# The GLU of branch A as a branch of the tail, and another order of the tail's branches

## The chip, the cores and the metric

The kernel runs on one core of one Trainium2 chip. The metric is device microseconds of one execution of the whole program. Three executions of the kernel before took 1948.1, 1957.22 and 1959.81 us (median 1957.22); a fourth was recorded by the hardware profiler and took 1951.2 us.

## The reference, cut to what matters

One layer of an encoder with four token mixers. `x` has 1024 prompt rows and 128 sample rows (T = 1152 together), 1024 columns, float32.

```python
h = split_cols(x @ p['w_in'])
ya, s5_re, s5_im = s5_branch(h['a_u'], p, st)         # A: state space, GELU, then the GLU below
yb, ... = dsa_branch(h, rel_bias, st)                 # B: sparse attention
yc, ... = gdn_branch(h, p, st)                        # C: gated DeltaNet
yd, ... = gla_branch(h, p, st)                        # D: GLA
branches = stack([ya * silu(a_gate), yb * silu(b_gate), yc * silu(c_gate), yd * silu(d_gate)])
proj  = einsum('ntbw,bwd->ntbd', branches, p['w_branch'])
gates = sigmoid(h['merge'])                           # (n, t, 4, 1024)
mixed = sum_b(gates * proj) @ p['w_out']
x = layer_norm(alpha * x + mixed)

# the end of s5_branch
y = gelu(y)                                           # (n, t, 512)
g = y @ p['s5_w_glu']                                 # (n, t, 1024)
ya = g[..., :512] * sigmoid(g[..., 512:])
```

## The kernel before, in words

Every product of two float32 matrices is made of three matmuls in a rounded format: `split` writes a rounded high part of a tile (ACT, L111 with a scale, L108 without) and the rest as a low part (DVE, L112 and L109), and `mm3` multiplies high by high (L188), high by low (L189) and low by high (L190). A product of a 128-column weight block with 384 tokens and 512 inner elements is thus 4 x 3 = 12 matmuls into one PSUM tile; the texts call it a **group**.

The tail starts when the projections are done. For each branch, `mix_branch` loads the branch's gated output `y_b` ... `y_a` from DRAM in three chunks of 384 tokens (tile `yl`, 768 KB each, two buffers), splits each into `YH` and `YL`, and then goes through eight blocks of 128 output columns: load and split a block of `w_branch` (`wst`, `whi`, `wlo`), three groups (`mix`, one for each chunk), and for each group a load of the merge gate (`mth`, three buffers), one DVE multiplication (L1769, or L1767 straight into the sum in the first branch) and one DVE addition into the sum `ACC` (L1770). Groups of one branch take their PSUM tiles in turn from two pools of two (`pg` and `pn`), so a group can start only when the one four before it was multiplied by DVE. One branch is 24 groups. The order of the branches is b, c, d, a; `finish` then multiplies the sum by `w_out` (`fin`) and normalises.

`YH` and `YL` have four places for chunks: one in the pool `y0`, opened early, three in `yb`. A branch's second and third chunk are split only when the branch before has used up a place, near its end.

`s5_glu` makes `y_a`. It reads the GELU output (`s5_y`, 512 x 1152) in four loads of 128 rows (`gy`), splits each with the tokens put in order on the way (`GH`, `GL`), and runs 24 groups (`glu`), two at a time (value and gate); ACT takes tanh of the gate (L1684), DVE combines twice (L1685, L1686), the second time with the branch's own gate (`glgt`), and the result is stored to `y_a`. Its tiles lie in pools on the right side of SBUF, where GLA (branch D) has its own until it ends.

The instructions are put in order by a scheduler that goes by priority: program order, with a class above it (`urgent`: loads and splits) and one below (`filler`). It decides while the program is built, so on the chip each engine and each DMA queue works its list strictly in order. GLA is still running through the first two branches of the tail: its last chunk of tokens goes through seven levels (`gla_levels`: DVE makes `X` and `glZ`, ACT an exponential, PE `lv` at L1208, DVE puts the result into `glAT` at L1211, after a first L1182), between `rms_gate` (L1062, PE `py` at L1065, DVE `oyt` at L1067) of the chunk before and its own.

Almost all DMAs are issued by one engine's queue, SP, each in its place of the list: one that waits holds up all behind it.

Of the kernel before, what the change touches and what calls it, by code (L numbers as in the profile page):

```python
# [95 lines left out]
def pmt(K, name="pm"):  # L96
    return K.pm.tile([128, 512], F32, tag="pm", name=name)
# [6 lines left out]
def split(K, hi, lo, src, scale=None, eng=None):  # L104

    nc = K.nc
    if scale is None:
        nc.scalar.copy(hi, src)  # L108
        (eng or nc.vector).tensor_tensor(lo, src, hi.bitcast(F32), op=OP.subtract)  # L109
    else:  # L110
        nc.scalar.activation(hi, src, AF.Copy, scale=scale)  # L111
        nc.vector.scalar_tensor_tensor(lo, src, scale, hi.bitcast(F32), op0=OP.mult, op1=OP.subtract)  # L112
# [1541 lines left out]
                nc.sync.dma_start(dst, t[:n, d * 64:d * 64 + 64])  # L1654


def s5_glu(K):

    nc, tc, I = K.nc, K.tc, K.I
    with tc.tile_pool(name="glu1", bufs=1, side="right") as p1, tc.tile_pool(name="glu", bufs=2, side="right") as p, \  # L1660
            tc.tile_pool(name="wglu", bufs=2, side="right") as wg:
        GH = p1.tile([128, 4, T], F32R, name="GH")
        GL = p1.tile([128, 4, T], F32R, name="GL")
        for j in range(4):
            y = p.tile([128, 8, 144], F32, name="gy", bufs=3)
            nc.sync.dma_start(y.rearrange("p s k -> p (s k)"), K.YA[j * 128:j * 128 + 128])
            o = lambda x: x[:, j].rearrange("p (k s) -> p s k", s=8)
            split(K, o(GH), o(GL), y, scale=0.5)
        for j in range(4):
            wv = load_w(K, [(j * 128, 128, 0), (512 + j * 128, 128, 128)], 256, kt=4, src=I["s5_w_glu"], pool=wg, stage=wg)  # L1670
            hi, lo = wv
            for t0 in range(0, T, 384):
                s = slice(t0, t0 + 384)
                pp = []
                for a in range(2):
                    ps = pmt(K, "glu")
                    ca = slice(a * 128, a * 128 + 128)
                    for k in range(4):
                        mm3(nc, ps[:, :384], hi[:, k, ca], lo[:, k, ca], GH[:, k, s], GL[:, k, s], k == 0, k == 3)
                    pp.append(ps)  # L1680
                th = p.tile([128, 384], F32, name="glth")
                gt = p.tile([128, 384], F32, name="glgt")
                nc.sync.dma_start(gt, K.GD["a"][j * 128:j * 128 + 128, s])
                nc.scalar.activation(th, pp[1][:, :384], AF.Tanh, scale=0.5)  # L1684
                nc.vector.scalar_tensor_tensor(th, th, 1.0, pp[0][:, :384], op0=OP.add, op1=OP.mult)  # L1685
                nc.vector.scalar_tensor_tensor(th, th, 0.5, gt, op0=OP.mult, op1=OP.mult)  # L1686
                nc.sync.dma_start(K.YD["a"][j * 128:j * 128 + 128, s], th)


def s5(K):  # L1690
    nc, tc = K.nc, K.tc
    with tc.tile_pool(name="sp", bufs=1) as K.sp:
# [25 lines left out]
    gemm_t(K, w, K.XH, K.XL, evac)  # L1718


def mix_branch(K, n, br, yp, p):

    nc, I = K.nc, K.I
    YH, YL, W = [], [], []

    def load_y(c):
        pool = K.y0 if (3 * n + c) % 4 == 0 else yp
        YH.append(pool.tile([128, 4, 384], F32R, tag="YH", name="YH"))
        YL.append(pool.tile([128, 4, 384], F32R, tag="YL", name="YL"))
        src = K.YD[br].rearrange("(k p) t -> p k t", p=128)[:, :, c * 384:c * 384 + 384]  # L1730
        if n == 0 and c == 0:
            for k in (slice(0, 2), slice(2, 4)):
                y = K.ws.tile([128, 1024], F32, tag="wst", name="yl")[:, 0:768].rearrange("p (k t) -> p k t", k=2)
                nc.sync.dma_start(y, src[:, k])
                split(K, YH[c][:, k], YL[c][:, k], y, scale=0.5)
            return
        y = p.tile([128, 4, 384], F32, tag="yl", name="yl")
        d = nc.sync.dma_start(y, src)
        if n == 0:
            K.ydma = d  # L1740
        split(K, YH[c], YL[c], y, scale=0.5)

    def load(dt):
        W.append(load_w(K, [(dt * 128, 128, 0)], 128, kt=4, src=I["w_branch"][BR[br]]))
    with urgent(K):
        for c in range(3):
            load_y(c)
            if c < 2:
                load(c)
    c = 0  # L1750
    for dt in range(8):
        if n == 3:
            w_out_part(K, dt, p)
        if dt > 1:
            load(dt)
        hi, lo = W[dt]
        for t in range(3):
            s = slice(t * 384, t * 384 + 384)
            ps = (K.pg.tile([128, 512], F32, tag="pg", name="mix") if c % 2 else pnt(K, "mix"))[:, :384]
            c += 1  # L1760
            for k in range(4):
                mm3(nc, ps, hi[:, k], lo[:, k], YH[t][:, k], YL[t][:, k], k == 0, k == 3)
            th = p.tile([128, 384], F32, tag="mth", name="mth", bufs=3)
            nc.sync.dma_start(th, K.MD[br][dt][:, s])
            a = K.ACC[:, dt, s].bitcast(F32)
            if n == 0:
                nc.vector.scalar_tensor_tensor(a, th, 1.0, ps, op0=OP.add, op1=OP.mult)  # L1767
            else:
                nc.vector.scalar_tensor_tensor(th, th, 1.0, ps, op0=OP.add, op1=OP.mult)  # L1769
                nc.vector.tensor_tensor(a, a, th, op=OP.add)  # L1770


def tail(K):
    tc = K.tc
    with tc.tile_pool(name="mx", bufs=2) as p, tc.tile_pool(name="ap", bufs=1) as ap, \
            tc.tile_pool(name="yb", bufs=3) as yp:
        K.ACC = ap.tile([128, 8, T], F32R, name="ACC")
        s5_glu(K)
        K.wo = K.ctx.enter_context(tc.tile_pool(name="wo", bufs=1, side="right"))
        mix_branch(K, 0, "b", yp, p)  # L1780
        mix_branch(K, 1, "c", yp, p)
        mix_branch(K, 2, "d", yp, p)
        mix_branch(K, 3, "a", yp, p)
        finish(K, yp, p)


# [157 lines left out]
def build(ctx, tc, I, O, stages, dev=None):  # L1944
    K = Env()
    K.nc, K.tc, K.ctx, K.I, K.O = tc.nc, tc, ctx, I, O
    setup(K)
    K.GD = {b: K.dram.tile([512, T], F32, name=f"gate_{b}") for b in "abcd"}
    K.YD = {b: K.dram.tile([512, T], F32, name=f"y_{b}") for b in "abcd"}
    K.MD = {b: [K.dram.tile([128, T], F32, name=f"merge_{b}{j}") for j in range(8)] for b in "abcd"}  # L1950
    K.QD = K.dram.tile([768, T], F32, name="q_d")
    K.VD = K.dram.tile([T, 512], F32, name="gla_v")
    K.UD = K.dram.tile([512, T], F32, name="s5_u")
    K.YA = K.dram.tile([512, T], F32, name="s5_y")
    K.DQK = [K.dram.tile([128, T], F32, name=f"dqk{a}") for a in range(4)]
    K.CQ = [K.dram.tile([512, T], F32, name=f"cq{a}") for a in range(3)]
    K.gp = ctx.enter_context(tc.tile_pool(name="gp", bufs=2))
    K.ws = ctx.enter_context(tc.tile_pool(name="ws", bufs=2))
    K.wp = ctx.enter_context(tc.tile_pool(name="wp", bufs=2))
    with tc.tile_pool(name="xp", bufs=1) as K.xp, ExitStack() as wn, ExitStack() as nat:  # L1960
        K.wn = wn.enter_context(tc.tile_pool(name="wn", bufs=1, side="right"))
        K.wnp = nat.enter_context(tc.tile_pool(name="wnat", bufs=1, side="right"))
        load_x(K)
        with tc.tile_pool(name="cvc", bufs=1) as K.cvc:
            gdn_prepare(K)
            K.glmask = gla_masks(K)
            with tc.tile_pool(name="bp", bufs=1) as K.bp:
                with ExitStack() as cv:
                    natural_cols(K)
                    nat.close()  # L1970
                    project_q(K)

                    def between():
                        project_rest(K, "end" in stages)
                        wn.close()
                        K.cvp = cv.enter_context(tc.tile_pool(name="cvp", bufs=2, side="right"))
                        project(K, "end" in stages)
                    dsa(K, between)
            if "c" in stages:
                gdn(K)  # L1980
            gdn_conv_state(K)
            if "a" in stages:
                s5(K)
            if "end" in stages:
                K.y0 = ctx.enter_context(tc.tile_pool(name="y0", bufs=1, side="right"))
            if "d" in stages:
                gla(K)
    if "end" in stages:
        tail(K)
    elif "a" in stages:  # L1990
        s5_glu(K)
    if dev:
        dev(K)

# [16 lines left out]
```

## Time and profile before

| | us |
|---|---|
| profiled execution | 1951.2 |
| its span in the trace | 1949.4 |
| median of 3 other executions | 1957.22 |
| PE busy (matmuls) | 1826.5 (94%) |
| DVE busy | 1450.9 (74%) |
| ACT busy | 681.0 (35%) |
| `mix` matmuls | 1512.1 to 1841.3 |
| `glu` matmuls | 1688.1 to 1746.3 |
| `fin` matmuls | from 1841.3 |

Times inside the execution are microseconds from the start of the span. A window row gives, for a stretch, the busy time of each engine with the number of its instructions, then the clock granted to the matmul engine as a share of full speed (1.00 is 2.4 GHz, 0.50 is 1.2 GHz), the busy share of the 16 DMA engines and their GB/s. A busy matmul engine at half clock is still busy, so the number of matmuls in a window tells what was done. A timeline row gives start, duration, engine, line, operation, written tile <- read tiles; in brackets the idle time before it and what ended it.

### The profile page before, as it was taken

The numbers are of one execution on the slowest core, as the hardware profiler recorded it, in microseconds if no ns is written. First come the engines' busy times: TensorE is split into PE (matmuls) and PEld (weight loads), VectorE is DVE, ScalarE is ACT, GpSimd is POOL, SyncE is SP. The second block draws the span as 40 slices with busy tenths as digits, with TensorE's granted clock in tenths as the row PEclk, the third lists the DMA queues.
The fourth block names the chain that finished last, engine by engine and source line by source line (L and its number), as shares of the span: only waits on it lengthen the run. The fifth ranks groups of instructions, "written<-read, shape, count | busy, mean of one in ns | idle before, by whom it ended". The sixth has DMA issues, their size and how long they took to land.

```text
span 1949.4 us, 31176 instructions
## 1 busy us (share of the span) xinstructions
PE 1826.5 (94%) x10962; PEld 1711.5 (88%) x10962; DVE 1450.9 (74%) x3915; ACT 681.0 (35%) x1538; POOL 265.7 (14%) x297
## 2 busy tenths in 40 slices
PE   7999999999999999988889898888898999899997
PEld 7989999989888999888888787778888899899986
DVE  7289999944999995489740669977657889747676
ACT  4251111133666655264212333223532322412210
POOL 1110111210212110101111112212212000000000
PEclk9999999999999999999998999999999999899999
DMA  6322323223222222386334554444353544656522
GB/s 191 96 68 70 88 85 97 91 90 86 82 82 67 73 59 79 81 269 192 102 94 139 152 149 126 143 125 132 123 134 104 179 130 146 192 169 192 159 87 87
DMA packets 333386, 234.53 MB, mean 120 GB/s; under 512 B 70475, under 2 KB 315003, under 8 KB 333230
## 3 DMA queue, kind: packets, MB, share of 16 engines
q1 hardware_dynamic: 325358, 220.87, 38.6%
q10 hardware_dynamic: 7488, 10.62, 1.5%
q8 instruction: 87, 1.43, 0.3%
q0 software_dynamic: 384, 1.05, 0.2%
q14 instruction: 69, 0.57, 0.1%
HBM read 156.12 MB, written 76.35 MB: 119 GB/s over the span
## 4 chain that ended last, share of the span: by engine, by line
PE 34%; DVE 16%; DMA 5%; issue 4%; ACT 3%; POOL 1%; SPq 1%; DVEq 0%; POOLq 0%; ACTq 0%
PE pg L190 3%; PE pg L188 3%; PE pg L189 3%; PE mix L189 2%; PE mix L188 2%; PE mix L190 2%; PE fin L190 2%; PE fin L188 2%; PE fin L189 2%; PE lv L1208 1%; PE glu L189 1%; PE glu L190 1%; PE glu L188 1%; DMA P<-rows_d 1%; DVE glAT L1211 1%
## 5 line engine op out<-in xcount | busy, mean ns | idle before, releaser
L190 PE MATMUL pg<-XH,wlo 128*128 128x384 f32 x1648 | 566.6, 344 | 0.0
L188 PE MATMUL pg<-XH,whi 128*128 128x384 f32 x1648 | 564.6, 343 | 1.9 <-DVE gth L237 1.9
L189 PE MATMUL pg<-XL,whi 128*128 128x384 f32 x1648 | 565.8, 343 | 0.0
L188 PEld LDWEIGHTS pg<-XH,whi 128*128 128x128 f32 x1648 | 314.3, 191 | 5.8 <-DVE gth L237 2.4
L190 PEld LDWEIGHTS pg<-XH,wlo 128*128 128x128 f32 x1648 | 314.2, 191 | 3.9 <-issue 1.8
L189 PEld LDWEIGHTS pg<-XL,whi 128*128 128x128 f32 x1648 | 313.9, 190 | 4.0 <-issue 2.0
L108 ACT CAST whi<-wst 128x1024 fp32r<-128x1024 f32 (+2 forms) x121 | 109.2, 906 | 243.9 <-PE pg L189 122.5
L109 POOL TENSOR_TENSOR wlo<-wst,whi 128x1024 fp32r<-128x1024 f32 x44 | 109.3, 2485 | 371.2 <-ACT whi L108 345.0
L109 DVE TENSOR_TENSOR wlo<-wst,whi 128x512 fp32r<-128x512 f32 (+2 forms) x77 | 74.7, 974 | 83.6 <-ACT whi L108 82.1
L189 PE MATMUL mix<-YL,whi 128*128 128x384 f32 x384 | 130.6, 341 | 1.5 <-DVE YL L112 1.4
L188 PE MATMUL mix<-YH,whi 128*128 128x384 f32 x384 | 130.7, 341 | 0.8 <-ACT YH L111 0.6
L190 PE MATMUL mix<-YH,wlo 128*128 128x384 f32 x384 | 131.2, 342 | 0.0
L1716 ACT ACTIVATE mth<-pg 128x384 f32<-128x384 f32 x96 | 46.9, 488 | 151.7 <-PE pg L190 88.0
L391 DVE TENSOR_SCALAR_CACHE_REDUCE tkj<-mk,tk_c 128x384 bf16<-128x384 f32 (+6 forms) x112 | 90.9, 875 | 0.6
L391 DVE TENSOR_SCALAR_CACHE_REDUCE tkj<-tkh,tk_c 128x384 bf16<-128x384 bf16 (+6 forms) x112 | 90.9, 876 | 0.5
L189 PEld LDWEIGHTS mix<-YL,whi 128*128 128x128 f32 x384 | 72.4, 189 | 2.2 <-DVE YL L112 2.1
L188 PEld LDWEIGHTS mix<-YH,whi 128*128 128x128 f32 x384 | 72.3, 188 | 1.7 <-ACT YH L111 0.9
L714 DVE SCALAR_TENSOR_TENSOR cy<-rb,cw,cy 128x384 f32<-128x384 f32 (+1 forms) x108 | 70.8, 656 | 3.0 <-ACT cy L712 2.5
L190 PEld LDWEIGHTS mix<-YH,wlo 128*128 128x128 f32 x384 | 72.5, 189 | 0.2
L534 ACT ACTIVATE pr<-pr,sm 128x256 f32<-128x256 f32 (+7 forms) x72 | 53.6, 745 | 16.9 <-DVE sm L533 16.5
L501 POOL TENSOR_TENSOR mb<-BT,mk 128x512 f32<-128x512 f32 (+1 forms) x32 | 42.0, 1313 | 107.8 <-DVE mx L528 102.5
L190 PE MATMUL fin<-WOH,YL 128*128 128x512 f32 x144 | 56.0, 389 | 0.0
(632 smaller groups left out, 3786.2 us busy)
## 6 DMA issues: line engine op xcount, KB each, us to landing
wst<-in_w_in SPq DMA_DIRECT2D x80, 512.0 KB
wst<-in_w_branch SPq DMA_DIRECT2D x32, 256.0 KB
gk<-cq SPq DMA_DIRECT2D x27, 256.0 KB
merge_b<-mth SPq DMA_DIRECT2D x24, 192.0 KB
cq<-cy SPq DMA_DIRECT2D x24, 192.0 KB
merge_c<-mth SPq DMA_DIRECT2D x24, 192.0 KB
kq<-cq SPq DMA_DIRECT2D x18, 256.0 KB
merge_d<-mth SPq DMA_DIRECT2D x24, 192.0 KB
```

The source lines that it names most:

```text
L108: nc.scalar.copy(hi, src)
L109: (eng or nc.vector).tensor_tensor(lo, src, hi.bitcast(F32), op=OP.subtract)
L188: nc.tensor.matmul(ps, lh, rh, start=start, stop=False)
L189: nc.tensor.matmul(ps, lh, rl, start=False, stop=False)
L190: return nc.tensor.matmul(ps, ll, rh, start=False, stop=stop)
L391: nc.vector.tensor_scalar(junk[a % 2][:, :ns[a]], up[a] if bit > 15 else sc[a], cand[:, a:a + 1].bitcast(F32), None, op0=OP.is_ge, op1=OP.add,
L501: bias = nc.gpsimd.tensor_tensor(mbv, bt[:, 2 * jj:2 * jj + 2, ::-1][:, :, 256 - band:], mk[:, None, off:n].to_broadcast([128, 2, band]), ...
L534: nc.scalar.activation(p[:, r, 0:n], p[:, r, 0:n], AF.Exp, bias=sm[:, 2 + r:3 + r], scale=1.0, accum_out=sm[:, r:r + 1])
L714: nc.vector.scalar_tensor_tensor(yc, rb[:, i:i + c], K.cw[:, i * 12 + a:i * 12 + a + 1], yc, op0=OP.mult, op1=OP.add)
L1208: nc.tensor.matmul(ps[:, o:o + 128], x[:, j, z * 128:z * 128 + 128], Z[:, j, :, z * 64:z * 64 + 64], start=True, stop=True)
L1211: nc.vector.copy_predicated(right(AT[:, 0:m].rearrange("p i h t -> p (i h) t")), right(masks[l][:, None, :]).to_broadcast([128, 4 * m, 64 ...
L1716: nc.scalar.activation(th[:, :n], ps, AF.Tanh, scale=0.5)
```

## The change

The GLU is written as one more branch: it uses the four `YH`/`YL` places, the `yl`, `mth` and `gth` buffers, the weight buffers and the two PSUM pools that the branches use. The GELU output stays in its stored order of tokens within a chunk (t mod 8 outer, t div 8 inner), so a chunk is loaded by four DMAs of 128 rows x 8 pieces x 48 elements (192 bytes a piece) and split without reordering; the order is put right in the last DVE operation. Gate and value groups alternate by block: three gate groups, tanh of each kept, then three value groups. The order of the branches becomes b, c, GLU, a, d, and `w_out` is loaded during d.

```diff
-def s5_glu(K):
...
+def load_y(K, n, c, yp):
+    pool = K.y0 if (3 * n + c) % 4 == 0 else yp
+    return [pool.tile([128, 4, 384], F32R, tag=t, name=t) for t in ("YH", "YL")]
+
+def filler_psum(K, c, name):
+    return (K.pg.tile([128, 512], F32, tag="pg", name=name) if c % 2 else pnt(K, name))[:, :384]
+
+def s5_glu(K, n, yp, p):
+    nc, I = K.nc, K.I
+    Y, W = [], []
+    def load(x):
+        W.append(load_w(K, [((1 - x % 2) * 512 + x // 2 * 128, 128, 0)], 128, kt=4, src=I["s5_w_glu"]))
+    with urgent(K):
+        for c in range(3):
+            Y.append(load_y(K, n, c, yp))
+            y = p.tile([128, 4, 384], F32, tag="yl", name="gy")
+            for k in range(4):
+                nc.sync.dma_start(y[:, k].rearrange("p (s t) -> p s t", s=8),
+                                  K.YA[k * 128:k * 128 + 128].rearrange("p (s t) -> p s t", s=8)[:, :, c * 48:c * 48 + 48])
+            split(K, Y[c][0], Y[c][1], y, scale=0.5)
+            if c < 2:
+                load(c)
+    c = 0
+    th = [None] * 3
+    for x in range(8):
+        j = x // 2
+        if x > 1:
+            load(x)
+        hi, lo = W[x]
+        for t in range(3):
+            s = slice(t * 384, t * 384 + 384)
+            ps = filler_psum(K, c, "glu")
+            c += 1
+            for k in range(4):
+                mm3(nc, ps, hi[:, k], lo[:, k], Y[t][0][:, k], Y[t][1][:, k], k == 0, k == 3)
+            if x % 2 == 0:
+                th[t] = p.tile([128, 384], F32, tag="mth", name="glth", bufs=3)
+                nc.scalar.activation(th[t], ps, AF.Tanh, scale=0.5)
+                continue
+            gt = K.gp.tile([128, 384], F32, tag="gth", name="glgt")
+            nc.sync.dma_start(gt, K.GD["a"][j * 128:j * 128 + 128, s])
+            nc.vector.scalar_tensor_tensor(th[t], th[t], 1.0, ps, op0=OP.add, op1=OP.mult)
+            g = gt.rearrange("p (t s) -> p t s", s=8)
+            nc.vector.scalar_tensor_tensor(g, th[t].rearrange("p (s t) -> p t s", s=8), 0.5, g, op0=OP.mult, op1=OP.mult)
+            nc.sync.dma_start(K.YD["a"][j * 128:j * 128 + 128, s], gt)
...
-        s5_glu(K)
         K.wo = K.ctx.enter_context(tc.tile_pool(name="wo", bufs=1, side="right"))
         mix_branch(K, 0, "b", yp, p)
         mix_branch(K, 1, "c", yp, p)
-        mix_branch(K, 2, "d", yp, p)
+        s5_glu(K, 2, yp, p)
         mix_branch(K, 3, "a", yp, p)
+        mix_branch(K, 4, "d", yp, p, last=True)
         finish(K, yp, p)
```

The order that the scheduler makes of it differs from b's end to the end of a. DVE at the start of branch c, before (`mth` and `mix` tiles of one group share a number's neighbourhood: 17763 is c's first group, 17780 its second; `YL_18208` is the split of d's first chunk):

```order
L1769 SCALAR_TENSOR_TENSOR mth_17776<-mth_17776,mix_17763 128x384
...
L1769 SCALAR_TENSOR_TENSOR mth_17793<-mth_17793,mix_17780 128x384
...
L112 SCALAR_TENSOR_TENSOR YL_18208<-yl_18209,YH_18207 128x1536
...
L1067 SCALAR_TENSOR_TENSOR oyt_16555<-py_16550,dnorm_15544,dgt_16504 128x512
...
L1182 TENSOR_TENSOR glAT_16566<-ident_70,diag_16569 128x1024
```

The same place now (17297 is c's first group, 17314 its second; `YL_17742` is the split of the GLU's first chunk):

```order
L1784 SCALAR_TENSOR_TENSOR mth_17310<-mth_17310,mix_17297 128x384
...
L1067 SCALAR_TENSOR_TENSOR oyt_16555<-py_16550,dnorm_15544,dgt_16504 128x512
...
L112 SCALAR_TENSOR_TENSOR YL_17742<-gy_17743,YH_17741 128x1536
...
L1182 TENSOR_TENSOR glAT_16566<-ident_70,diag_16569 128x1024
...
L1211 COPY_PREDICATED glAT_16566<-lm3_400,lv_16621 128x64x8
...
L1784 SCALAR_TENSOR_TENSOR mth_17327<-mth_17327,mix_17314 128x384
L1211 COPY_PREDICATED glAT_16566<-lm4_411,lv_16634 128x32x16
```

The multiplication of c's second group, which stood before GLA's `oyt` and L1182, now stands behind four of its levels.

SP at the end of the GLU, now (`glgt_18171`, `18189`, `18207` are the last three results, one for each chunk; `yl_18214`, `18226`, `18238` are the chunks of `y_a` for branch a):

```order
L1737 DMA y_a_91<-glgt_18171 128x384
L1779 DMA mth_18255<-merge_a0_95 128x384
L1737 DMA y_a_91<-glgt_18189 128x384
L1755 DMA yl_18214<-y_a_91 128x4x384
L1755 DMA yl_18226<-y_a_91 128x4x384
L181 DMA wst_18403<-in_w_branch 128x4x128
L1733 DMA glgt_18207<-gate_a_87 128x384
L1779 DMA mth_18272<-merge_a0_95 128x384
L1737 DMA y_a_91<-glgt_18207 128x384
L1779 DMA mth_18289<-merge_a0_95 128x384
L1755 DMA yl_18238<-y_a_91 128x4x384
```

Before, the same stores and loads stood beside branch d's remaining seven blocks; now branch a's loads follow the last store, and no group of another branch stands between them on PE.

PE at the end of the GLU, now (18194 is its last group; 18242, 18259 and 18276 are branch a's first block with its three chunks, 18293 the second block with the first chunk):

```order
L190 MATMUL glu_18194<-YH_17771,wlo_18153 128x384
L188 MATMUL mix_18242<-YH_18212,whi_18218 128x384
...
L188 MATMUL mix_18259<-YH_18224,whi_18218 128x384
L188 MATMUL mix_18293<-YH_18212,whi_18230 128x384
L189 MATMUL mix_18259<-YL_18225,whi_18218 128x384
...
L188 MATMUL mix_18276<-YH_18236,whi_18218 128x384
```

Before, 21 groups of branch d stood between the last `glu` matmul and the first of branch a.

## Rows read from the trace of the kernel before

**Rows 1.** The page, busy time of each engine over the span.
```profile
PE 1826.5 (94%) x10962; PEld 1711.5 (88%) x10962; DVE 1450.9 (74%) x3915; ACT 681.0 (35%) x1538; POOL 265.7 (14%) x297
```

**Rows 2.** Windows of the tail: PE, PEld, DVE, ACT, POOL, clock, DMA, GB/s.
```profile
1614.00:1648.00 34.00, 33.47 (x213) 31.99 (x212) 32.82 (x75) 7.26 (x12) 0.00 (x0) 1.00 0.49 147
...
1750.00:1787.00 37.00, 37.00 (x212) 37.00 (x211) 23.70 (x45) 3.96 (x7) 0.00 (x0) 1.00 0.58 188
```

**Rows 3.** Windows around the first matmuls of the GLU, same columns.
```profile
1683.00:1689.00 6.00, 3.02 (x12) 2.04 (x11) 3.32 (x3) 4.70 (x5) 0.00 (x0) 0.81 0.93 305
1689.00:1694.00 5.00, 5.00 (x19) 5.00 (x18) 4.27 (x3) 2.18 (x1) 0.00 (x0) 0.55 0.64 217
1694.00:1697.00 3.00, 2.37 (x14) 2.05 (x12) 0.69 (x1) 2.86 (x3) 0.00 (x0) 1.00 0.30 110
1697.00:1700.00 3.00, 1.43 (x7) 1.12 (x7) 2.90 (x2) 2.28 (x2) 0.00 (x0) 1.00 0.85 262
1700.00:1704.00 4.00, 4.00 (x16) 4.00 (x16) 3.29 (x4) 0.00 (x0) 0.00 (x0) 0.57 0.30 104
```

**Rows 4.** Waits of PE from 1500 on: total us, times, longest.
```profile
PE glu L188 <- ACT GH L111: 1.8, 2, 1.1
PE glu L189 <- DVE GL L112: 1.4, 1, 1.4
```

**Rows 5.** Timeline of SP: issues at three places of the tail.
```profile
1611.12 0.37 SPq L1738 DMA_DIRECT2D yl<-y_d  x1
...
1680.62 0.51 SPq L1666 DMA_DIRECT2D gy<-s_y  x1
...
1740.02 0.32 SPq L1687 DMA_DIRECT2D y_a<-glth  x1
...
1741.89 0.37 SPq L1738 DMA_DIRECT2D yl<-y_a  x1
...
1744.18 0.32 SPq L1687 DMA_DIRECT2D y_a<-glth  x1
```

**Rows 6.** Timeline of DVE through GLA's last chunk at the start of branch c.
```profile
1614.35 0.54 DVE L1769 SCALAR_TENSOR_TENSOR mth<-mth,mix 128x384 f32<-128x384 f32 x1
...
1616.30 0.55 DVE L1769 SCALAR_TENSOR_TENSOR mth<-mth,mix 128x384 f32<-128x384 f32 x1
...
1617.22 1.76 DVE L112 SCALAR_TENSOR_TENSOR YL<-yl,YH 128x1536 fp32r<-128x1536 f32 x1 [0.30 <-ACT YH L111]
...
1623.20 0.75 DVE L1067 SCALAR_TENSOR_TENSOR oyt<-py,dnorm,dgt 128x512 f32<-128x512 f32 x1 [0.34 <-PE py L1065]
...
1625.34 1.22 DVE L1182 TENSOR_TENSOR glAT<-ident,diag 128x1024 f32<-128x1024 f32 x1
...
1639.93 0.72 DVE L1211 COPY_PREDICATED glAT<-lm,lv 128x512 f32<-128x512 uint8 x1
```

**Rows 7.** Timeline of PE in the same stretch.
```profile
1622.54 0.63 PE L1065 MATMUL py<-ident,glo 128*128 128x128 f32 x4 [0.16 <-DVE glo L1062]
...
1626.46 0.42 PE L190 MATMUL mix<-YH,wlo 128*128 128x384 f32 x1
...
1631.81 1.13 PE L1208 MATMUL lv<-glZ,X 128*128 128x128 f32 x8 [0.38 <-DVE X L1203]
```

**Rows 8.** DMA queues from 11 to 15 us, where three loads of short rows run.
```profile
DMA packets 3160, 0.63 MB, mean 156 GB/s; under 512 B 3097, under 2 KB 3097, under 8 KB 3160
...
q1 hardware_dynamic: 3160, 0.63, 91.0%
```

**Rows 9.** Timeline of ACT and DVE around the first load of `y_a`.
```profile
1743.01 0.55 DVE L1685 SCALAR_TENSOR_TENSOR glth<-glth,glu 128x384 f32<-128x384 f32 x1 [3.01 <-ACT glth L1684]
1743.60 0.56 DVE L1686 SCALAR_TENSOR_TENSOR glth<-glth,glgt 128x384 f32<-128x384 f32 x1
...
1746.37 1.49 ACT L111 ACTIVATE YH<-yl 128x1536 fp32r<-128x1536 f32 x1 [3.39 <-DMA yl<-y_a]
...
1747.89 1.76 DVE L112 SCALAR_TENSOR_TENSOR YL<-yl,YH 128x1536 fp32r<-128x1536 f32 x1 [3.73 <-ACT YH L111]
```

More of the change, by code (lines that the diff above doesn't have):

```diff
@@ L1654, in s5_states_out @@
                 nc.sync.dma_start(dst, t[:n, d * 64:d * 64 + 64])
-def s5_glu(K):
[L1659 to L1687, printed above, removed]
 def s5(K):
@@ L1718, in merge_cols @@
     gemm_t(K, w, K.XH, K.XL, evac)
-def mix_branch(K, n, br, yp, p):
-    nc, I = K.nc, K.I
[L1724 to L1729, printed above, removed]
+def load_y(K, n, c, yp):
[3 more added lines that the diff above has]
+    return (K.pg.tile([128, 512], F32, tag="pg", name=name) if c % 2 else pnt(K, name))[:, :384]
@@ L1730, in load_y, with mix_branch, load_part @@
+def mix_branch(K, n, br, yp, p, last=False):
+    nc, I = K.nc, K.I
+    Y, W = [], []
+    def load_part(c):
+        Y.append(load_y(K, n, c, yp))
         src = K.YD[br].rearrange("(k p) t -> p k t", p=128)[:, :, c * 384:c * 384 + 384]
@@ L1734, in load_y @@
                 nc.sync.dma_start(y, src[:, k])
-                split(K, YH[c][:, k], YL[c][:, k], y, scale=0.5)
+                split(K, Y[c][0][:, k], Y[c][1][:, k], y, scale=0.5)
             return
         y = p.tile([128, 4, 384], F32, tag="yl", name="yl")
[L1738 to L1741, printed above, removed]
+        nc.sync.dma_start(y, src)
+        split(K, Y[c][0], Y[c][1], y, scale=0.5)
     def load(dt):
@@ L1746, in mix_branch @@
         for c in range(3):
-            load_y(c)
+            load_part(c)
             if c < 2:
@@ L1751, in mix_branch @@
     for dt in range(8):
-        if n == 3:
+        if last:
             w_out_part(K, dt, p)
@@ L1758, in mix_branch @@
             s = slice(t * 384, t * 384 + 384)
-            ps = (K.pg.tile([128, 512], F32, tag="pg", name="mix") if c % 2 else pnt(K, "mix"))[:, :384]
+            ps = filler_psum(K, c, "mix")
             c += 1
             for k in range(4):
-                mm3(nc, ps, hi[:, k], lo[:, k], YH[t][:, k], YL[t][:, k], k == 0, k == 3)
+                mm3(nc, ps, hi[:, k], lo[:, k], Y[t][0][:, k], Y[t][1][:, k], k == 0, k == 3)
             th = p.tile([128, 384], F32, tag="mth", name="mth", bufs=3)
@@ L1989, in build @@
         tail(K)
-    elif "a" in stages:
-        s5_glu(K)
     if dev:
```

## The prediction

> **What bounds the kernel now.** I read the page's busy times first: PE has 1826.5 us of work in a span of 1949.4 us [rows 1], no other engine comes near. The windows of the tail come next. From 1750 to 1787 PE is never idle, at full clock, and 212 matmuls take 37.00 us: 0.174 us each, 2.1 us for a group of 12 [rows 2]. That is the pace to hold other stretches against. From 1614 to 1648, where GLA's last chunk runs beside branch c, PE still has work 33.47 of 34 us, but DVE is full too, 32.82 us [rows 2]: an order that hurts either engine costs time there. One place of the tail is clearly off the pace, the GLU's start from 1683 to 1704: 68 matmuls in 21 us [rows 3]. The waits say for what: the `glu` matmuls wait for the splits GH on ACT and GL on DVE [rows 4], and SP shows why those are late, the first `gy` is asked for only at 1680.62 [rows 5], after GLA has given up the right side of SBUF.
>
> Three terms follow: one gone, two new. All are times of PE, since it is the engine that runs out last.
>
> **1. The GLU's start, gone.** 68 matmuls at 0.174 us are 11.8 us; they took 21, so 9.2 us were lost. Of these 5.2 us are idle (6, 5, 3, 3, 4 us less the busy 3.02, 5.00, 2.37, 1.43, 4.00) and 4.0 us are clock: after the first idle stretch the granted clock is 0.55 from 1689 to 1694, after the second 0.57 from 1700 to 1704, half of full speed for most of it [rows 3]. Now the GLU's chunks use the branches' places; the second and third are split in the 6.3 us of c's last three groups, each 1.49 us on ACT and 1.76 on DVE [rows 9], so the GLU starts as any branch does. The matmuls are as many as before (24 groups), so are the weight loads; the splits shrink from four strided ones to three like a branch's, in place of d's. **Minus 9.2 us.**
>
> **2. The start of branch c, new.** The order puts the split of the GLU's first chunk and four levels of GLA ahead of the multiplication of c's second group. Before, that group is multiplied at 1616.30, and about a dozen mix and weight operations of DVE stand between 1614.35 and 1639.93 [rows 6]. Now: without the two groups and the split of `y_d` (1.76 us from 1617.22) in front of it, `oyt` comes when PE has done `py`, some 4.5 us earlier than 1623.20, at 1618.7; three updates of the state, 1.1 us, then the split, 1.76 us, then a weight split, bring L1182 to 1623.1 instead of 1625.34 [rows 6]. From L1182 to the fifth level's L1211 it is 14.6 us before [rows 6]; about 3 us of that are mix and weight operations that now stand later, so c's second group is multiplied near 1634.8. Four groups can be on PE until then. They end so: the second and most of the third by 1618.0, then GLA's `py` to the first `lv`, 3.9 us (1622.54 to 1626.46 [rows 7]), then the rest of the third, the fourth and the fifth, 26 matmuls or 4.5 us: 1626.5. From there to 1634.8 PE has three `lv` of 1.13 us [rows 7] and nothing else: 8.3 less 3.4 is 4.9 us idle, in pieces of about 2. Clock: in term 1 the first stretch lost 2.6 us to the clock (31 matmuls in 11 us are 5.6 us lost, 3.0 of them idle), the second 1.4 (37 in 10 us, 3.6 lost, 2.2 idle) [rows 3]; I take 2.0. Bounds: 0, if GLA's own matmuls and a shorter chain fill the gap (rows 2 show 0.5 us of idle now, with the same work in another order), to 11, the whole 8.3 and 2.6. I take 6.9, nearer the middle, since the order leaves PE no other group. **Plus 6.9 us.**
>
> The twelve loads of 192-byte pieces stand on SP in front of c's other `mth` loads and GLA's `dgt` and `dv`. Their price: from 11 to 15 us three loads of such short rows run, 3160 packets of 199 bytes on average, engines busy 91% [rows 8]; 0.91 x 4 us x 16 / 3160 is 18.4 ns a packet, so 1024 packets on 16 engines take 1.2 us. The first chunk's four take over the place on SP of the `y_d` load at 1611.12 [rows 5] and wait once for a weight buffer; they are there by 1618, split on ACT by 1619.5, a microsecond before DVE gets to them; the third chunk's, behind that split, let the second `mth` land near 1630, before 1634.8. By the row they cost nothing beside the order. The Trainium skill speaks against this shape: "DMA: Bandwidth & Descriptors", Specifications, wants at least 512 bytes for line rate and says that below this the engine does a read-modify-write. The trace agrees as far as it goes: 156 GB/s in rows 8 against 305 in rows 3. If rows 8 hold the whole of that cost, the sum stays; if each packet moved twice on top of it, the loads would double and the sum rise by 3.4 us (third rival).
>
> **3. From the GLU to branch a, new.** a's input is the GLU's result through DRAM, and PE's order has only a behind the GLU; d, ready long before, stands last. Counting from the end of the group that completes the first chunk: DVE combines and the store goes out after 1.2 us (1743.01 to 1744.18 [rows 5, 9]). The load of the first chunk stands behind the store of the second, whose group ends 2.1 us later: 3.3. A load waits only 1.87 us after its store (1740.02 to 1741.89 [rows 5]), which is over by then; it goes out at 3.7. To ACT it takes 4.48 us (1741.89 to 1746.37), then 1.52 to DVE's start and 1.76 there [rows 5, 9]: 11.5. PE ended the GLU at 4.2, so it idles 7.3 us, and the clock falls as after the first stretch of term 1, 2.6 us. The third chunk is later still: its combination stands on DVE behind the first chunk's split, 12.0, then 1.87, 4.48, 3.28 and some queueing, 21.8; PE has three groups until then, 6.3 us, and at a lower clock 8.9, from 11.5 to 20.4, and one more group of the second chunk to put behind the first matmul of the third. So its lateness and the clock cover each other; a full clock would cost 2.2 us there instead. Bounds: 5, if the load takes 2.6 us (768 KB at the 305 GB/s of [rows 3]) and the clock stays, to 14, if the third chunk adds its wait to the slow clock. **Plus 9.9 us.**
>
> Edits that cost nothing: the new last DVE operation reads with a stride, but DVE has room even beside a branch (23.70 of 37 us [rows 2]); the four-place rotation frees d's places during a; `w_out` moves from a to d with the same cover; `lng` and `lnb` load earlier.
>
> **Sum.** -9.2 + 6.9 + 9.9 = +7.6 us. Against the profiled execution, 1951.2 us (span 1949.4), that is 1958.8. That execution lies 6.0 under the median of the three others, 1957.22, which spread over 11.7 us; the mean of all four is 1954.1, and I set the forecast on it: **1962 us**.
>
> **Rivals.**
> - *The start of c costs nothing.* DVE and GLA's levels shift so that PE's four groups last; for it speaks that PE loses nothing there now with DVE as full [rows 2], against it the order. -9.2 + 9.9: 1955.
> - *Not slower.* As above, and the round trip takes its lower bound, 5: the mechanism is a load that runs alone at 305 GB/s instead of the 4.48 us measured beside other loads. -9.2 + 5.0 = -4.2: 1950. It decides when term 3 stays under 9.2 with term 2 at nothing. Against it: two loads of 768 KB and one of `glgt` go out together.
> - *Short pieces decide; slower.* At twice the 18.4 ns the first chunk's loads end at 1611.1 + 9.4 + 1.9 (the last part as for a store), ACT takes 1.5, the split on DVE begins at 1623.9 instead of 1620.5, 3.4 us late, GLA and the second group with it: 1965. At three times it is 8.2 us, and the third chunk's loads then hold the second `mth` past DVE's need by 3.5: +19.3, 1973; from 3.5 times on it is more than 1% slower. For it speaks that rows 8 are reads of weights at an idle time, against it that they have the same mean size.
> - *The release still binds.* The GLU's start keeps its 9.2 us because another place is not free in time: 1971. Against it: c and d start without loss in the same places.
>
> **How the numbers follow.** About 1% (19.6 us) is what a measurement of this kernel can tell from no change. Forecast 0.50, start of c free 0.19, not slower 0.15, short pieces 0.12, release 0.04. The range for 8 in 10 goes from the not-slower case to three-times-dear short pieces: 1947 to 1974. More than 1% faster would need 19.6 us where only 9.2 are to be had beside about 3 us of scattered idle: 0.02. More than 1% slower comes from short pieces beyond 3.5 times, or both new terms at their upper bounds (-9.2 + 11 + 14 = 15.8, so 1970) with the pieces somewhat dear: 0.10. The rest, 0.88, is within 1%.
>
> **What would show it.** Right: the windows around the first `glu` matmul at full pace and clock; PE idle some 5 us while L1211 runs at c's start; after the last `glu` matmul an idle stretch of 7 us ending on YL, and a clock near 0.5 behind it; `gy` loads near 1.2 us each. Wrong: no gap at either place; DVE waiting for `gy` or `mth`; the GLU waiting for its splits again.

## The result, and the profile after

The changed kernel took 1967.34 us (median of 10 runs, 1963.38 to 1977.49) against 1954.86 us for the kernel before in the same sets (10 runs, 1944.03 to 1960.69). The ratio is 1.0072, 95% interval 1.0053 to 1.0090: 14.1 us slower, from 10.4 to 17.6, where +7.6 us had been forecast. The profiled execution took 1963.38 us with a span of 1961.6, 12.2 more than before.

The page of the changed kernel has PE's work unchanged, as in [rows 1]; what grew is the time beside it:

```profile
PE 1827.8 (93%) x10962; PEld 1712.9 (87%) x10962; DVE 1453.6 (74%) x3914; ACT 675.6 (34%) x1537; POOL 266.3 (14%) x297
```

Windows of the changed kernel's tail, columns as in [rows 2]. Behind the windows one figure is used through this whole part: **what PE lost** in a window is its length less busy time times granted clock, so both idle time and half clock count.

```profile
1612.00:1624.00 12.00, 11.97 (x78) 11.57 (x77) 10.19 (x25) 2.21 (x3) 0.00 (x0) 1.00 1.11 190
1624.00:1630.00 6.00, 2.58 (x11) 1.98 (x10) 4.49 (x10) 1.26 (x2) 0.00 (x0) 0.77 1.17 274
1630.00:1636.00 6.00, 2.75 (x11) 2.51 (x12) 4.37 (x12) 0.69 (x2) 0.00 (x0) 0.50 0.01 3
1636.00:1642.00 6.00, 6.00 (x28) 6.00 (x27) 4.05 (x10) 1.32 (x3) 0.00 (x0) 0.59 0.09 20
...
1688.00:1738.00 50.00, 50.00 (x286) 50.00 (x285) 23.42 (x35) 10.67 (x21) 0.00 (x0) 1.00 0.37 117
1738.00:1744.00 6.00, 1.47 (x9) 1.15 (x7) 2.00 (x3) 0.62 (x1) 0.00 (x0) 0.94 0.77 234
1744.00:1750.00 6.00, 3.06 (x8) 2.66 (x9) 2.30 (x2) 2.97 (x2) 0.00 (x0) 0.50 0.63 210
1750.00:1756.00 6.00, 6.00 (x26) 5.65 (x26) 4.01 (x6) 0.00 (x0) 0.00 (x0) 0.71 0.61 189
1756.00:1762.00 6.00, 4.29 (x25) 3.96 (x24) 3.52 (x5) 2.97 (x2) 0.00 (x0) 1.00 0.67 217
```

Where the GLU's start was off the pace [rows 3], 286 matmuls now take 50 us without a gap (1688 to 1738): the first term is gone as forecast. Two places are new: c's start from 1624 to 1642, and the way from the GLU to branch a from 1739 to 1760. PE's waits from 1500 us on (total, times, longest) name both; the splits GH and GL of [rows 4] are not among them any more:

```profile
PE lv L1208 <- DVE X L1203: 10.0, 7, 2.8
PE mix L188 <- ACT YH L111: 9.0, 3, 6.4
...
PE mix L189 <- DVE YL L112: 1.1, 1, 1.1
```

(The first of these was 3.3 us in 4 times before, the second 0.6 in one.)

**The start of c.** DVE's timeline in the changed kernel, answering to [rows 6]; `YL<-gy` is the GLU's first chunk, the two L1784 are the multiplications of c's first and second group:

```profile
1612.13 0.55 DVE L1784 SCALAR_TENSOR_TENSOR mth<-mth,mix 128x384 f32<-128x384 f32 x1
...
1618.12 1.74 DVE L112 SCALAR_TENSOR_TENSOR YL<-gy,YH 128x1536 fp32r<-128x1536 f32 x1
...
1621.55 1.22 DVE L1182 TENSOR_TENSOR glAT<-ident,diag 128x1024 f32<-128x1024 f32 x1
...
1629.45 0.69 DVE L1211 COPY_PREDICATED glAT<-lm,lv 128x512 f32<-128x512 uint8 x1 [0.78 <-PE lv L1208]
...
1633.26 0.69 DVE L1211 COPY_PREDICATED glAT<-lm,lv 128x512 f32<-128x512 uint8 x1 [1.56 <-PE lv L1208]
...
1635.74 0.55 DVE L1784 SCALAR_TENSOR_TENSOR mth<-mth,mix 128x384 f32<-128x384 f32 x1
...
1637.38 0.71 DVE L1211 COPY_PREDICATED glAT<-lm,lv 128x512 f32<-128x512 uint8 x1 [1.10 <-PE lv L1208]
```

PE in the same stretch, answering to [rows 7]:

```profile
1627.37 2.05 PE L1208 MATMUL lv<-glZ,X 128*128 128x128 f32 x8 [2.83 <-DVE X L1203]
1631.18 2.05 PE L1208 MATMUL lv<-glZ,X 128*128 128x128 f32 x8 [1.77 <-DVE X L1203]
1635.30 2.04 PE L1208 MATMUL lv<-glZ,X 128*128 128x128 f32 x8 [2.08 <-DVE X L1203]
```

The split of `gy` waits for no load (nothing in brackets), and of DVE's waits from 1611 to 1646 us (4.3 us for `lv`, 0.8 for `py`, 0.7 and 0.6 for ACT) none is for a load. Between c's first and second multiplication lie 23.6 us, 1.95 before. PE has its four groups done at 1624.4 and then waits for GLA's levels; after the first wait the clock is at half, an `lv` takes 2.05 us in place of 1.13, and DVE, which needs it, waits in turn.

**From the GLU to a.** SP's issues in the changed kernel, answering to [rows 5], at both places:

```profile
1608.89 2.12 SPq L1710 DMA_DIRECT2D gy<-s_y  x3
...
1612.06 4.74 SPq L1710 DMA_DIRECT2D gy<-s_y  x5
...
1625.71 15.04 SPq L1779 DMA_DIRECT2D mth<-merge_c  x4
...
1738.87 0.32 SPq L1737 DMA_DIRECT2D y_a<-glgt  x1
1739.29 1.88 SPq L1755 DMA_DIRECT2D yl<-y_a  x2
...
1741.76 0.51 SPq L1733 DMA_DIRECT2D glgt<-gate_a  x1
...
1750.31 0.32 SPq L1737 DMA_DIRECT2D y_a<-glgt  x1
...
1752.18 0.37 SPq L1755 DMA_DIRECT2D yl<-y_a  x1
```

ACT there, answering to [rows 9]:

```profile
1744.30 1.48 ACT L111 ACTIVATE YH<-yl 128x1536 fp32r<-128x1536 f32 x1 [4.31 <-DMA yl<-y_a]
...
1757.01 1.48 ACT L111 ACTIVATE YH<-yl 128x1536 fp32r<-128x1536 f32 x1 [7.39 <-DMA yl<-y_a]
```

and DVE:

```profile
1739.58 0.56 DVE L1734 SCALAR_TENSOR_TENSOR glth<-glth,glu 128x384 f32<-128x384 f32 x1 [0.73 <-PE glu L190]
...
1749.45 0.83 DVE L1736 SCALAR_TENSOR_TENSOR glgt<-glth,glgt 128x384 f32<-128x384 f32 x1 [1.88 <-DMA glgt<-gate_a]
```

The GLU's last group is done at 1739.3. Its second combination (L1736) runs only at 1749.45: its branch gate was asked for at 1741.76, behind the two loads of `y_a` (768 KB each), and took 7.7 us. So the third chunk is stored at 1750.31, loaded at 1752.18, and PE, idle again, starts on it at 1758.54:

```profile
1758.54 0.62 PE L188 MATMUL mix<-YH,whi 128*128 128x384 f32 x2 [1.72 <-ACT YH L111]
```

What PE lost from 1600 to 1860 us, added up from windows of 2 us (those with under 0.15 us left out), for the kernel before, the changed one and the eight experiments below. Matmuls whose result nothing reads are counted as lost. The last column is the ratio of the times to the kernel before, with its 95% interval.

| | c's start | GLA's end | GLU's start | GLU to a | other | sum, against before | time, against before |
|---|---|---|---|---|---|---|---|
| before | 0.5 | - | 9.9 | - | 0.4 | 10.8 | |
| changed | 11.7 | - | - | 12.5 | - | 24.2, +13.4 | +14.1 (1.0053 to 1.0090) |
| 1: d between GLU and a | 11.6 | 0.3 | - | - | 1.9 | 13.9, +3.1 | +3.3 (1.0000 to 1.0033) |
| 2: GLU's loads held | 1.0 | 3.1 | - | 13.8 | 0.3 | 18.2, +7.4 | +5.7 (1.0012 to 1.0047) |
| 3: both | 1.0 | 2.8 | - | - | 1.9 | 5.7, -5.1 | -6.7 (0.9951 to 0.9980) |
| 4: PE busy before a | 11.6 | 0.2 | - | 11.1 | 0.4 | 23.3, +12.5 | +12.9 (1.0042 to 1.0090) |
| 5: third gate buffer | 11.8 | 1.3 | - | 10.2 | 0.3 | 23.6, +12.8 | +11.9 (1.0038 to 1.0083) |
| 6: 4 and 5 | 11.7 | 0.2 | - | 10.3 | 0.8 | 23.0, +12.2 | +15.1 (1.0050 to 1.0103) |
| 7: 3 with long rows | - | 2.1 | - | - | 1.1 | 3.2, -7.6 | -3.1 (0.9967 to 1.0001) |
| 8: PE busy in the levels | 11.3 | - | - | 13.1 | 0.3 | 24.7, +13.9 | +12.9 (1.0043 to 1.0090) |

In nine of nine kernels the sum of what PE lost in the tail lies within 5 us of the measured difference, in seven within 2. That is what licenses reading the losses stage by stage. How much one stage varies from profile to profile shows where the list is the same: c's start loses 11.6 to 11.8 us in the changed kernel and experiments 1, 4, 5 and 6, the way from the GLU to a 12.5, 13.8 and 13.1 in the changed kernel and experiments 2 and 8.

### The profile page after: what moved, and what is told of

It reads as the page before. It is cut to its first block, busy times and chain, and to the rows that moved or that the text cites. A ratio compares the mean times of both kernels' runs of the same rounds, so it can differ in the third digit from the quotient of the medians.

```text
span 1961.6 us, 31183 instructions
## 1 busy us (share of the span) xinstructions
PE 1827.8 (93%) x10962; PEld 1712.9 (87%) x10962; DVE 1453.6 (74%) x3914; ACT 675.6 (34%) x1537; POOL 266.3 (14%) x297
## 4 chain that ended last, share of the span: by engine, by line
PE 36%; DVE 14%; DMA 6%; issue 3%; ACT 2%; POOL 1%; SPq 1%; DVEq 0%; POOLq 0%; ACTq 0%
PE pg L188 4%; PE pg L190 4%; PE pg L189 4%; PE mix L188 3%; PE mix L189 3%; PE mix L190 3%; PE fin L190 2%; PE fin L189 2%; PE fin L188 2%; PE lv L1208 1%; DMA P<-rows_d 1%; PE glu L190 1%; PE glu L188 1%; PE glu L189 1%; DVE glAT L1211 1%
## 5 line engine op out<-in xcount | busy, mean ns | idle before, releaser
L534 ACT ACTIVATE pr<-pr,sm 128x256 f32<-128x256 f32 (+7 forms) x72 | 53.6, 745 | 17.1 <-DVE sm L533 16.7
L1784 DVE SCALAR_TENSOR_TENSOR mth<-mth,mix 128x384 f32<-128x384 f32 x72 | 39.2, 551 | 25.7 <-PE mix L190 16.1
```

Of the source, the lines that this page charges most:

```text
L534: nc.scalar.activation(p[:, r, 0:n], p[:, r, 0:n], AF.Exp, bias=sm[:, 2 + r:3 + r], scale=1.0, accum_out=sm[:, r:r + 1])
```

## The experiments

**1. d between the GLU and a.** The changed kernel with its last two branches exchanged.

```diff
         s5_glu(K, 2, yp, p)
-        mix_branch(K, 3, "a", yp, p)
-        mix_branch(K, 4, "d", yp, p, last=True)
+        mix_branch(K, 3, "d", yp, p)
+        mix_branch(K, 4, "a", yp, p, last=True)
```

> Only the last two branches change places: b, c, GLU, d, a. The start of c keeps the changed kernel's order of instructions word for word. Theory (two places cost time: c's start 11.0 us, the way from the GLU to branch a 13.0 us, against 9.2 us won at the GLU's start): the 13.0 us go, because 24 groups of d stand between the last store of the GLU's result and its first use; 13 us faster than the changed kernel, about 2 us slower than the kernel before (ratio 1.000 to 1.002), and the window behind the last glu matmul at full pace. Rival 1 (the 192-byte pieces cost the time, wherever they run): unchanged, 14 us slower than before. Rival 2 (c's start costs nothing on balance, the round trip is all of it): 23 us faster than the changed kernel, 9 us faster than before.

Ratio to before 1.0017 (1.0000 to 1.0033), 3.3 us; the changed kernel has 14.1. Its windows at c's start and behind the GLU:

```profile
1630.00:1636.00 6.00, 3.14 (x18) 2.85 (x17) 5.51 (x10) 1.05 (x2) 0.00 (x0) 0.91 1.04 217
1636.00:1642.00 6.00, 3.44 (x15) 2.88 (x14) 3.38 (x8) 0.83 (x2) 0.00 (x0) 0.50 0.35 125
...
1744.00:1750.00 6.00, 6.00 (x36) 6.00 (x35) 5.96 (x6) 2.98 (x3) 0.00 (x0) 1.00 0.73 208
```

The loss behind the GLU is gone and the one at c's start is the same to 0.1 us. The round trip through DRAM is thus worth the 12.5 us that the windows say, less a new wait of 1.5 us in branch d (at 1762). Both rivals fail: "short pieces" had no gain here, "c's start is free" a kernel 9 us faster than before.

**2. The GLU's first load held back.** Order and pieces of the changed kernel; the first `gy` load is ordered behind the seventh merge-gate load of c.

```diff
-                nc.sync.dma_start(y[:, k].rearrange("p (s t) -> p s t", s=8),
-                                  ...)
+                d = nc.sync.dma_start(y[:, k].rearrange("p (s t) -> p s t", s=8),
+                                      ...)
+                if c == k == 0:
+                    issue_after(K, d, K.mths[30])
...
-            nc.sync.dma_start(th, K.MD[br][dt][:, s])
+            K.mths.append(nc.sync.dma_start(th, K.MD[br][dt][:, s]))
```

> The changed kernel's order of branches, and the same twelve loads of 192-byte pieces, but the first of them is held in the list behind the seventh merge-gate load of branch c, so that the scheduler again puts the multiplications of c's second and third group ahead of the GLA levels that follow. Theory (the order of DVE at c's start costs 11.0 us there): 9 to 11 us faster than the changed kernel, 3 to 5 us slower than before (ratio 1.002); from the start of c to GLA's end PE has no idle stretch over 1 us and the clock stays 1.00. Rival (short pieces): they are all still there, no gain.

Ratio 1.0029 (1.0012 to 1.0047), 5.7 us slower than before, 8.4 faster than the changed kernel. Windows at c's start:

```profile
1630.00:1636.00 6.00, 5.58 (x33) 5.26 (x31) 5.97 (x13) 1.89 (x3) 0.00 (x0) 1.00 0.40 118
1636.00:1642.00 6.00, 5.50 (x35) 5.08 (x35) 5.73 (x14) 1.16 (x2) 0.00 (x0) 1.00 0.09 31
```

and SP:

```profile
1619.05 2.23 SPq L1710 DMA_DIRECT2D gy<-s_y  x3
...
1622.22 1.55 SPq L1781 DMA_DIRECT2D mth<-merge_c  x3
...
1646.74 4.90 SPq L1710 DMA_DIRECT2D gy<-s_y  x5
```

Of the 11.7 us at c's start 1.0 is left, at full clock. All twelve loads of short pieces are still in the kernel, but only three of them at c's start: the held one and those behind it go out from 1646.74 on. So the edit moved two lists, DVE's and SP's, and prices them together. In the changed kernel the merge gate of c's second group goes out at 1625.71, behind all twelve loads; with the 4.0 us that it takes here from issue to use (1622.22 to 1626.26) it is there at 1629.7. This is an estimate, and by it SP's list alone would have left PE without a group of c for some 5 us (from 1624.4) in any order of DVE. That DVE multiplies only at 1635.74 is its own list's doing. That the cost is order and not the pieces' transfers rests on this experiment together with DVE's waits at c's start, none of which is for a load. How much either list costs alone was not run.

The gain is 0.6 us under the range expected. At a new place, GLA's end from 1658 to 1668, 3.1 us are lost where the expectation had seen nothing.

**3. Both edits.** 2 and 1 together; no further line is changed.

> Both edits together: the GLU's first load held behind c's merge-gate loads, and b, c, GLU, d, a. Theory: both losses go and the gain at the GLU's start stays: 7 to 9 us faster than before (ratio 0.995 to 0.9965). Rival (short pieces): at or above the kernel before. If the two losses are one and the same slack counted twice, the gain over the changed kernel is that of the better single edit, some 13 us, and the time that of the kernel before.

Ratio 0.9966 (0.9951 to 0.9980): 6.7 us faster than the kernel before and 20.8 faster than the changed one, the sum of the two single gains (10.8 and 8.4) within 2 us. This version beats both kernels. It falls 0.3 us short of the range expected; 2.8 us at GLA's end and 1.9 elsewhere are what it still loses.

**4. PE kept busy before branch a.** The changed kernel with 36 matmuls behind the last `glu` group that nothing reads.

```diff
             nc.sync.dma_start(K.YD["a"][j * 128:j * 128 + 128, s], gt)
+    for r in range(3):
+        ps = pmt(K, "spare")[:, :384]
+        for k in range(4):
+            mm3(nc, ps, hi[:, k], lo[:, k], Y[2][0][:, k], Y[2][1][:, k], k == 0, k == 3)
```

> The changed kernel with 36 more matmuls of 128x384 behind the last glu group, whose result nothing reads (3 groups over the GLU's last chunk, 6.3 us at full clock): they fill the gap before branch a and keep the clock up. The slow clock behind the gap costs PE 3.9 us of the 13.0. Theory A (the third chunk of y_a sets the end of the stretch: its first matmul can start at 1758.5 whatever the clock, and PE has only 36 matmuls before it): no change against the changed kernel, within 1 us; the idle time moves to the place before the third chunk, some 4 to 5 us there. Theory B (idle time and clock add up, as the sum of the prediction had it): 3 to 4 us faster than the changed kernel.

Ratio 1.0066 (1.0042 to 1.0090), which cannot be told from the changed kernel's 1.0072. The windows behind the last `glu` matmul:

```profile
1740.00:1752.00 12.00, 12.00 (x70) 12.00 (x69) 4.07 (x6) 1.60 (x3) 0.00 (x0) 1.00 0.63 188
1752.00:1760.00 8.00, 6.11 (x33) 5.40 (x32) 6.03 (x6) 3.01 (x3) 0.00 (x0) 1.00 0.56 180
1760.00:1766.00 6.00, 2.99 (x18) 2.66 (x17) 2.15 (x3) 1.85 (x2) 0.00 (x0) 1.00 0.94 324
```

The clock stays at 1.00 all through, and 4.9 us are idle again, 3.0 of them from 1762 on: PE now arrives early and waits for the third chunk. The stretch loses 11.1 us in place of 12.5 (4.9 and 36 spare matmuls of 0.174), so at most 1.3 of the 3.3 us that the windows put down to the half clock came back. That is no more than the stretch varies by with the changed kernel's list (12.5 to 13.8), and the third chunk came 0.9 us earlier here, counted from the first load of `y_a` (18.4 us to PE's first matmul of it, 19.2 in the changed kernel). Theory A.

**5. A third gate buffer.** The changed kernel; the gates of the GLU's results get a pool of three.

```diff
-            gt = K.gp.tile([128, 384], F32, tag="gth", name="glgt")
+            gt = K.g3.tile([128, 384], F32, name="glgt")
...
-        s5_glu(K, 2, yp, p)
+        with tc.tile_pool(name="g3", bufs=3, side="right") as K.g3:
+            s5_glu(K, 2, yp, p)
```

> The changed kernel with three buffers of their own for the branch gate (glgt) instead of the two shared ones: the gate of the third chunk's last result is asked for ahead of the two loads of y_a and not behind them, so that the third chunk's store no longer waits for it. Theory A (the third chunk of y_a sets the end of the stretch): its load goes out some 4.5 us earlier, when the first chunk's split gives its yl buffer back; its first matmul can start near 1754 instead of 1758.5, but now the 36 matmuls that PE has before it end only at 1756.6 at the slow clock: the stretch from the last glu matmul to pace gets 1.5 to 2.5 us shorter, from 12.5 us lost to about 10.5. Theory B (the first chunk's round trip and the clock set it): nothing changes, 12.5 us lost.

SP at the end of the GLU in this kernel:

```profile
1750.65 1.88 SPq L1755 DMA_DIRECT2D yl<-y_a  x2
...
1753.17 0.48 SPq L1737 DMA_DIRECT2D y_a<-glgt  x1
...
1760.76 0.37 SPq L1755 DMA_DIRECT2D yl<-y_a  x1
```

The third chunk's store now follows the loads of the other two by 2.5 us; in the changed kernel it was 11.0 (1739.29 to 1750.31). The third load goes out 10.1 us behind the first ones, 12.9 before, and the stretch loses 10.2 us, where A said 10.5 and B 12.5: the gate's wait for the loads ahead of it was worth 2.3 us against the changed kernel's profile, and more against the other two with its list (13.8 and 13.1). The interval of the ratio, 1.0061 (1.0038 to 1.0083), is too wide to show that.

**6. Third gate buffer and busy PE.** Edits 4 and 5 together.

> The third gate buffer and the 36 matmuls that nothing reads, together. Theory A: with the third chunk there early, the slow clock is no longer covered by its lateness, so keeping PE busy is worth something now where alone it was worth 1.2 us at most: PE has its 36 real matmuls done near 1754 and goes on with the third chunk then; the stretch loses about 8 us, the spare matmuls counted as lost, 4 to 5 less than the changed kernel (8 to 10 us slower than before). Theory B: the two edits do no more together than alone, 11 us lost.

Ratio 1.0077 (1.0050 to 1.0103), and 10.3 us lost in the stretch: A had 8, B 11. A's number failed. SP shows another transfer ahead of the third chunk's:

```profile
1763.25 0.33 SPq L1824 DMA_DIRECT2D lng<-in_ln_g  x1
1763.70 0.37 SPq L1759 DMA_DIRECT2D yl<-y_a  x1
```

In this kernel's list the load of `lng` (512 KB) stands ahead of the third chunk's, whose data reach ACT 6.5 us after the issue (1763.70 to 1770.21) where experiment 5 had 4.6 (1760.76 to 1765.35). That `lng` is what made the difference, and that the two edits would give 8 us without it, was not run.

**7. Both edits, long rows.** As 3, with as many bytes and loads, but rows of 1536 bytes; the tokens of the GLU then come in another order.

```diff
-                d = nc.sync.dma_start(y[:, k].rearrange("p (s t) -> p s t", s=8),
-                                      ...)
+                d = nc.sync.dma_start(y[:, k], K.YA[k * 128:k * 128 + 128, c * 384:c * 384 + 384])
```

> The kernel of both edits (GLU's first load held, b, c, GLU, d, a), but each of the twelve GLU loads fetches 128 rows of 1536 bytes in place of 1024 pieces of 192 bytes: as many bytes, as many DMAs, other tokens (the GLU's tokens are left unsorted, so what it computes is put in other places). The first load is held behind the same merge-gate load; the scheduler then moves one multiplication of c ahead of GLA's step. Theory (the pieces cost nothing of their own, they only changed the order): same as the kernel of both edits within 2 us, 5 to 9 us faster than before. Rival (the pieces cost by themselves): 4 us or more faster than the kernel of both edits.

Ratio 0.9984 (0.9967 to 1.0001), against 0.9966 (0.9951 to 0.9980) with the short pieces: not faster, by the medians slower. The tail lost 3.2 us in its profile instead of 5.7, so a price of the pieces of up to 2 or 3 us stays open. The two kernels differ in one thing more: three multiplications of c stand ahead of GLA's `oyt` here, two in experiment 3. As far as that is worth little (1.0 us is lost at c's start there, nothing here), the 4 us and more of the rival are excluded.

**8. PE kept busy in GLA's levels.** The changed kernel; `lv` of three levels at c's start is made three times.

```diff
+        for r in range(2 if i == 6 and 0 < l < 4 else 0):
+            spare = pmt(K, "spare")
+            for z in range(m):
+                for j in range(2):
+                    o = (2 * z + j) * 128
+                    nc.tensor.matmul(spare[:, o:o + 128], x[:, j, z * 128:z * 128 + 128], Z[:, j, :, z * 64:z * 64 + 64],
+                                     start=True, stop=True)
```

> The changed kernel, with the matmuls of GLA's levels 1, 2 and 3 at the start of c made three times over, the second and third time into a tile that nothing reads: 2.3 us of PE work behind each of these lv, where PE is idle 1.8 to 2.8 us before the next one. DVE's order around it is the changed kernel's up to the multiplication of c's second group; the third group's stands one level later. In the changed kernel an lv takes 2.05 us there at half clock instead of 1.13, and the next steps of DVE wait for it. Theory A (the slow clock lies on the chain DVE - lv - DVE, and lengthens the very stretch that it comes from): with PE kept busy the clock stays at 1.00 and from one L1211 to the next it takes 3.2 to 3.5 us instead of 3.8 to 4.3; c's second group is multiplied some 2 us earlier, the losses at c's start, the spare matmuls counted as lost, fall from 11.7 us to 7 to 9, and the time is 2 to 4 us under the changed kernel's (ratio to before 1.005 to 1.0062). Theory B (DVE alone sets the pace of that stretch, PE's clock is only seen in it): the spacing and the time stay as in the changed kernel.

DVE in this kernel (L1218 is the changed kernel's L1211, L1791 its L1784):

```profile
1629.73 1.22 DVE L1182 TENSOR_TENSOR glAT<-ident,diag 128x1024 f32<-128x1024 f32 x1
...
1636.86 0.69 DVE L1218 COPY_PREDICATED glAT<-lm,lv 128x512 f32<-128x512 uint8 x1
...
1639.76 0.71 DVE L1218 COPY_PREDICATED glAT<-lm,lv 128x512 f32<-128x512 uint8 x1 [0.47 <-PE lv L1208]
...
1641.57 0.55 DVE L1791 SCALAR_TENSOR_TENSOR mth<-mth,mix 128x384 f32<-128x384 f32 x1
...
1642.96 0.73 DVE L1218 COPY_PREDICATED glAT<-lm,lv 128x512 f32<-128x512 uint8 x1 [0.18 <-PE lv L1208]
```

The clock stays at 1.00 until 1648. From level to level DVE takes 2.90 and 3.20 us, 3.81 and 4.12 in the changed kernel, and from L1182 to c's second multiplication 11.8 us against 14.2. So the half clock does lie on the chain. The time does not show it (1.0066, 1.0043 to 1.0090): the spare matmuls are 6.1 us, and 3.7 us are lost from 1646 to 1654, where c's third group now stands a level later. Theory A holds for the mechanism and fails for the sum, 11.3 us lost where it said 7 to 9.

## Why the prediction was right, and where it was too small

Its case (both new losses, the GLU's start won) is the one that came; the time lies in its range, 5 us above the forecast. The difference was +14.1 us and not +7.6, which lies below the measured interval (10.4 to 17.6): both new terms were too small.

- **Term 1**, -9.2: right. The windows of the kernel before give 9.9 lost there, the changed kernel nothing.
- **Term 2**, +6.9: the place and the cause, the order, are right (experiment 2, with SP's list moved along), the size is not: 11.7 less the 0.5 of before is 11.2. Counted from c's first multiplication, PE runs out of groups where the working had it (after 12.2 us), but the second multiplication comes after 23.6 us, not 20.5. The step that failed is "PE has three `lv` of 1.13 us". They took 2.05, since the clock had already fallen in the idle stretch ahead of them. I had priced the clock only as slower work of PE (2.0 us) and had left it out of the chain that makes PE wait. DVE needs each `lv` to go on: 14.2 us from L1182 to the second multiplication, where the working had 11.7, and experiment 8 shows 11.8 once the clock stays up. Idle time became 7.1 us (forecast 4.9), the clock's part 4.6 (2.0). The upper bound given, 11, is the right number by luck: it was made of 8.3 us idle and 2.6 of clock.
- **Term 3**, +9.9: place and cause right (experiment 1), size 12.5. The first chunk came almost as worked out: its split ended at 1747.6, 12.5 us after its group (1735.1), where I had 11.5; the load took 5.0 us to ACT (1739.29 to 1744.30), not 4.48. The step that failed is the 21.8 us of the third chunk, with which "its lateness and the clock cover each other". They do cover each other, as experiment 4 shows, but the lateness was larger: the split of the third chunk ended 25.2 us after that group (at 1760.3), PE stood idle for 1.7 us ahead of it, and the clock cost 3.3 us in place of 2.6. Its combination stood at 1749.45, 14.3 after that group, where I had 12.0, because the last branch gate waited on SP behind the two 768 KB loads. That load was in the list that I had read; I had counted it on DVE and not in the DMA queue. DVE waited 1.9 us for it; experiment 5 prices it at 2.3 us or more.
- **Short pieces**: "by the row they cost nothing beside the order" holds within the 2 to 3 us that experiment 7 leaves. In the changed kernel's profile from 1612 to 1619 us, with five of the loads:

```profile
DMA packets 6715, 1.43 MB, mean 205 GB/s; under 512 B 6203, under 2 KB 6715, under 8 KB 6715
...
q1 hardware_dynamic: 6715, 1.43, 135.6%
```

  That is 22.6 ns of packet time each (1.356 x 7 us x 16 / 6715) against 18.4 worked out from [rows 8]. The share is above 100%, so packets overlapped: one passed an engine every 16.7 ns (7 us x 16 / 6715). Neither is near double. The rate, 205 GB/s, is low beside the 305 of [rows 3]. That agrees with "DMA: Bandwidth & Descriptors" of the Trainium skill (Specifications), which wants 512 bytes or more for line rate; no term followed from it.
- **Rivals**: "start of c free" and "not slower" fall with experiment 1, "release still binds" with the windows of the GLU.
- **Level**: set on 1954.1 for the kernel before, measured 1954.86; nothing of the miss lies there.

## What to carry to other kernels

Where an engine's idle stretch ends in a wait for a chain that the same engine's small steps are part of, price those steps at the lower clock and walk the chain again: here the chain was 2.4 us longer for it (14.2 against 11.8), of the 4.3 us between 6.9 and 11.2. Where a stage stores to DRAM what the next one loads, look for another stage to put between them in program order: putting d between the GLU and a gave back 10.8 us for two lines. When a load of another shape joins a list that a scheduler orders, look first at what it moved: holding the first load back gave 8.4 us with the pieces unchanged in size.

## What the runs showed of the hardware

- In the changed kernel issuing a load of 1024 pieces of 192 bytes took SP 0.52 to 1.49 us (median 0.67), a 768 KB load in long rows 0.37: the twelve took 9.6 us of SP's list with the short gaps between them. What that cost by itself was not run.
- A 192 KB load took 7.7 us from issue to use behind two 768 KB loads and a weight load on the same queue (`glgt`, 1741.76 to 1749.45).
- The stage ahead of the tail varies more than the effects studied: the first `mix` matmul started between 1510.5 and 1520.3 us in six profiled executions (before, changed, experiments 1, 2, 3 and 7) whose lists are the same up to there. Losses added up by stage met the times to 2 us in seven of nine kernels, where the interval of a time spans 6 to 10 us.
